# A joined softmax minimum, a third engine for the softmax scale, uneven last pieces and a different warm-up in a two-layer streaming encoder

## The chip, the cores and the metric

The kernel runs on one core of a Trainium2 chip. The core has TensorE (PE in the profile, with its weight loads listed apart as PEld), VectorE (DVE), ScalarE (ACT), GpSimd (POOL), SyncE (SP), whose queue issues all DMAs here, and 16 DMA engines between HBM and the on-chip memory SBUF. TensorE writes its results to the accumulator memory PSUM, which DVE and ACT read. The metric is device time in microseconds, the median of several runs; a profiled execution has its own time and, inside it, the span from the first to the last instruction.

## The reference

One step of a two-layer encoder for 2048 prompt frames and 32 sample frames, all in float32 with 1024 channels. Layer 0 projects the normalised input to queries, keys, values and gates of two attention branches. Branch A has 8 query heads on 2 key heads, sees its own chunk of 64 frames and the two before, and has a learned sink per head; branch B has 8 heads, sees its own chunk and the eight before, and adds a learned bias:

```python
    s = jnp.einsum('bqhgd,bshd->bhgqs', q, k).astype(jnp.float32) * (dh ** -0.5)
    if bias_table is not None:
        s = s + bias.reshape(kvh, g, tq, tk)
    if sinks is not None:
        m = jnp.maximum(jnp.max(s, axis=-1, keepdims=True), sink)
        p = jnp.exp(s - m)
        p = p / (jnp.sum(p, axis=-1, keepdims=True) + jnp.exp(sink - m))
    else:
        p = jax.nn.softmax(s, axis=-1)
    return jnp.einsum('bhgqs,bshd->bqhgd', p.astype(v.dtype), v)
...
    y = jnp.concatenate([oa.reshape(b, t, -1) * jax.nn.silu(ga),
                         ob.reshape(b, t, -1) * jax.nn.silu(gb)], axis=-1)
    return y @ w_out
```

Layer 1 projects to a recurrent branch and a gate, applies a short convolution, a gated linear recurrence along time and an output projection. After each layer comes `x + rms_norm(y) * g`. The outputs are both streams and the new caches and states.

## The kernel before

Data is kept channel-major: channels on the 128 partitions in eight groups, time along the columns. The 2084 columns are cut into six column tiles (five of 352, one of 324), which are handled in three pairs. A dense product multiplies a weight tile of 1024 by 128 with a column tile. For accuracy every operand is split into a high and a low part of reduced precision, and three products (high-high, high-low, low-high) are summed, 24 matmuls for one output tile. Weights come in by DMA (`wst`) and are split on chip: `w_split` (line 485) copies the high part on ACT or DVE and subtracts to get the low part on DVE or POOL (lines 491 to 499). The weights of layer 0's output projection are named wo0.

Attention works in units of 128 queries (32 for the sample). `soft` (line 1231) makes one unit: score products into one of the two PSUM buffers `S`; `reduce` (line 1242), one fused DVE operation a piece, which subtracts the scores from the bias or mask, writes the negated scores to `pt` and keeps their minimum in `nm` (the largest score, negated); the exponent with its sum on ACT (line 1279); a reciprocal on DVE; and the scale of `pt` by the reciprocal and by 0.5 on DVE or POOL (lines 1290 to 1293). The 0.5 belongs to the gate: SiLU is computed as half of `(tanh(z/2) + 1) * z`, and the kernel leaves the half out of the gate and puts it here. In branch B a unit has up to 640 key columns; with five key tiles the scores are two pieces of 320 columns in two buffers, each with its own minimum, and a DVE operation on one column (line 1257) takes the smaller. The sample's units of branch B are two pieces of 272. In branch A a unit has four heads of up to 256 columns, each with its own minimum, which starts from the sink; its scale is four operations. After the scale, TensorE transposes `pt` into the PSUM buffers `T`, ACT copies the high part to `pp`, DVE subtracts for the low part, TensorE multiplies with the values into `O`, and ACT and DVE empty it.

The order of all instructions on all engines is written out by a planner inside the kernel (class `Sched`, lines 166 to 395). Every piece of work is a generator that yields requests: the engine, or a choice of engines with costs in microseconds, and the data and buffers that it needs. The planner keeps a modelled clock for each engine, takes requests by priority, places one on an engine when that engine is modelled to be free within 0.6 us (`LOOK`) and the data is there, and among several engines takes the earliest modelled finish (`pick`, line 323). The dense products have the lowest priority on TensorE and fill what attention leaves. On the chip each engine then runs its list in that order. From the end of attention on, `sch.alone` keeps POOL out of every choice for long stretches.

Layer 1's output projection, `out_part` (line 1730), ends in `fin_out` (line 1629): ACT scales a finished output tile into `m` and squares it, the squares are summed, TensorE sums them over the partitions, ACT takes the root, DVE the reciprocal, and then `m` is multiplied by it and the residual `xt` is added, in channel groups of five and three, on DVE or POOL; SP stores. In the very last column tile the last output tile is computed in two pieces of 162 columns (line 1761), each with its own norm, so that the first piece's norm runs while the second is multiplied.

At the start TensorE multiplies ones by ones eight times (lines 1584 to 1585) before the first data arrives.

Of the kernel before, what the change touches and what calls it, by code (L numbers as in the profile page):

```python
# [12 lines left out]
OP = mybir.AluOpType  # L13
# [38 lines left out]
NQT = 3  # L52
WIN = 3.4133


# [343 lines left out]
def hybrid_kernel(ctx, tc, I, O):  # L399
# [85 lines left out]
    def w_split():  # L485
        for i in range(1, len(WSEQ)):
            if not fresh[i]:
                continue
            wcur[1] = i
            w_use()  # L490
            e, (h, l) = yield R(("A", "V"), [("wst", i), lambda: sch.w.get(wst[i].tensor.name)], [whr, wlr], cost=(0.95, 0.6))
            sch.set(("wt", i))
            s = wst.pop(i)
            if e == "A":
                A.copy(h, s)
            else:
                V.tensor_copy(h, s)
            e, _ = yield R(("V", "G"), [h], cost=(1.14, 2.3))
            ENG[e].tensor_tensor(l, s, f32(h), OP.subtract)
            wstr.release(s)  # L500
            wt[i] = (h, l)
            wleft[i] = 1 if WSEQ[i][0] in ("w0", "wo0") else 2
            if wleft[i] == 2:
                spawn(w_keep(i), PWK)
            sch.set(("W", i), sch.w[l.tensor.name])
# [725 lines left out]
    def soft(run, np_, groups, out, sink=None):  # L1231
# [9 lines left out]

        def reduce(ps, pieces, o0):
            yield R("V", [ps] + ex)
            o = 0
            for i, (_, ks, bv, j) in enumerate(pieces):
                n = ks.stop - ks.start
                V.tensor_tensor_reduce(out=pt[:np_, o0 + o:o0 + o + n], in0=ps[:np_, o:o + n], in1=bv, scale=-1.0,
                                       scalar=BIG if sink is None else nsk[:np_, sink + j:sink + j + 1],
                                       op0=OP.add, op1=OP.min, accum_out=nm[:np_, j:j + 1])
                o += n  # L1250
            Sr.release(ps)
            left[0] -= 1
            if not left[0]:
                if run.bias is not None:
                    run.b_done()
                if sink is None and len(groups) == 2:
                    V.tensor_tensor(nm[:np_, 0:1], nm[:np_, 0:1], nm[:np_, 1:2], OP.min)
                if sink is not None:
                    V.tensor_tensor(r[:np_], sk[:np_, sink:sink + 4], nm[:np_], OP.add)
                sch.set(uid, sch.t["V"] + 0.13)  # L1260

        for gi, pieces in enumerate(groups):
# [5 lines left out]
            for qs, ks, _, _ in pieces:  # L1268
# [3 lines left out]
                o += n  # L1272
            spawn(reduce(ps, pieces, o0), PT)
            o0 += o
# [14 lines left out]
        n = sum(x[1] for x in out)  # L1289
        e, _ = yield R(("V", "G"), [r], cost=(0.06 + n * 0.00053, 0.1 + n * 0.00106))  # L1290
        for j, (o, w) in enumerate(out):
            x = pt[:np_, o:o + w]
            ENG[e].tensor_scalar(x, x, r[:np_, j:j + 1], 0.5, OP.mult, OP.mult)
        for g, t in ((nmr, nm), (smr, ss), (rr4, r)):
# [288 lines left out]
    sch.set(("wst", 1))  # L1583
    for _ in range(NWARM):
        PE.matmul(warmp[:, 0:128], ones, ones, start=True, stop=True)
    psr_.release(warmp)
    spawn(w_first(), -3)
# [33 lines left out]
    class Out:  # L1621


        def __init__(self, b, bi, residual, gi, dst, final):
            self.b, self.bi, self.residual, self.gi, self.dst, self.final = b, bi, residual, gi, dst, final
            self.m = self.sa = None
            self.n, self.left = 0, 2

    def fin_out(S, c, acc, rel, cs):
# [23 lines left out]
        m, half = S.m, S.final and S.bi == 1  # L1653
        pieces = [(o, sw) for o, sw in subs(blk) if cs.start <= o < cs.stop]
        xg = xtr if S.final else xrr
# [16 lines left out]

        def add(o, sw, tm):

            cc = slice(o, o + sw)
            for ks in parts:
                nk = ks.stop - ks.start
                e, _ = yield R(("V", "G"), [lambda: tm[ks.start], lambda: S.xk.get(o)], cost=(0.2 * nk, (FG if S.final else 0.42) * nk))
                xt = S.xt[o]
                ENG[e].tensor_tensor(m[:, ks, cc], m[:, ks, cc], xt[:, ks, :sw], OP.add)  # L1680
                tm[ks.start] = sch.t[e] + 0.13
                if half or ks.stop == KT:
# [4 lines left out]
                                 in_=m[:, sk_, cc])  # L1687
            S.xg.release(xt)
            x2n[S.dst is x2T, S.b] = x2n.get((S.dst is x2T, S.b), 0) + 1
# [6 lines left out]

        for o, sw in pieces:
            cc, tm = slice(o, o + sw), {}
            yield R("V", [r])
            V.reciprocal(r[:, cc], r[:, cc])  # L1700
            for ks in parts:
                nk = ks.stop - ks.start
                e, _ = yield R(("V", "G"), [r], cost=(0.2 * nk, 0.42 * nk))
                ENG[e].tensor_tensor(m[:, ks, cc], m[:, ks, cc], r[:, None, cc].to_broadcast([128, nk, sw]), OP.mult)
                tm[ks.start] = sch.t[e] + 0.13
            spawn(add(o, sw, tm), 0)
        rg.release(r)

    def res_load(S):

        S.xg = xtr if S.final else xrr
        S.xt, S.xk = {}, {}
        for o, sw in subs(2 * S.b + S.bi):
            xt, = yield R("SP", rings=[S.xg])
# [15 lines left out]
    def out_part(b, base, ri, residual, gi, dst, ykey, late=False, late_m=False, final=False):  # L1730
# [7 lines left out]
        for n, (c, bi, wi) in enumerate(order):  # L1738
# [20 lines left out]
            if final and n == 15:  # L1759

                for o, sw in subs(2 * b + bi):
                    if o:
# [359 lines left out]
```

## Time and profile before

| | |
|---|---|
| runs | 1827.22, 1828.31, 1827.37 us; median 1827.37 |
| the profiled execution's own time | 1823.5 us |
| its span | 1821.7 us |
| busy: PE, DVE, ACT, POOL | 1731.5, 1555.3, 996.5, 326.5 us |
| mean granted TensorE clock | 0.988 of full speed |

All lines of a profile carry the line number of one helper (L101), so work is told apart by the names of its tiles: `acc` is a dense product's accumulator; `r0h`, `r0l`, `r1h`, `r1l` are the high and low parts of the activations, `wh` and `wl` of the weights; `S`, `T`, `O`, `pt`, `nm`, `pp` are as above; `rr` holds the reciprocals, `ssm` the sums, `sacc` and `tz` or `tzb` the sums of squares and squares of the norm, `misc` its product over the partitions. The fused reduce is listed as CUSTOM_DVE_ANT_0, followed by a read of its accumulator. Shapes are partitions x elements. In a group's line the first number after the bar is the busy time in us, the second the mean ns of one instruction, and after the second bar stands the engine's idle time before it with what ended it.

### The profile page before, as it was taken

To read this page: it belongs to the slowest core of one execution; us is meant where nothing else is said; L and a number is where in the kernel's file an instruction comes from. 1 tells how busy PE (TensorE), PEld (TensorE's weight loads), DVE (VectorE), ACT (ScalarE), POOL (GpSimd) and SP (SyncE) were. 2 spreads that over 40 slices of the span, in tenths; PEclk is the share of its full clock that TensorE was granted. 3 is DMA by queue.
4 is the path that set the end of the run, shared out by engine and by line. 5 is a ranking of instruction groups with operands and counts; after the bars stand their busy time and mean duration, and the time that the engine had idled before them with its cause. 6 is when DMAs were issued, how large, how long until landed. Compare 5 with 4: busy or idle time off the path is not lost.

```text
span 1821.7 us, 31694 instructions
## 1 busy us (share of the span) xinstructions
PE 1731.5 (95%) x11078; PEld 1671.8 (92%) x11078; DVE 1555.3 (85%) x3330; ACT 996.5 (55%) x2037; POOL 326.5 (18%) x284
## 2 busy tenths in 40 slices
PE   8999999999999999999998999998999999999995
PEld 7999999998999999899997999998999899999995
DVE  9899967899998779998988789899999988798843
ACT  4275543476666416665565344457753675447831
POOL 4332204323322233311222000000011000100002
PEclk8999999999999999999998999999999999999998
DMA  5788766888654368877764985684566735575376
GB/s 179 203 245 265 228 190 196 226 232 237 192 149 141 97 186 248 210 217 195 216 194 122 278 248 168 210 267 147 217 213 217 204 124 174 165 208 171 128 268 193
DMA packets 293576, 362.80 MB, mean 199 GB/s; under 512 B 36308, under 2 KB 244616, under 8 KB 293400
## 3 DMA queue, kind: packets, MB, share of 16 engines
q1 hardware_dynamic: 293416, 360.78, 66.5%
q8 instruction: 87, 1.43, 0.3%
q14 instruction: 73, 0.60, 0.1%
HBM read 255.77 MB, written 107.00 MB: 199 GB/s over the span
## 4 chain that ended last, share of the span: by engine, by line
PE 49%; DVE 29%; DMA 9%; ACT 6%; issue 4%; SPq 1%; POOL 1%; DVEq 0%; ACTq 0%; POOLq 0%
PE acc L101 35%; PE T L101 4%; PE O L101 4%; PE S L101 4%; DVE pt L101 3%; DVE ex L101 3%; DVE m L101 3%; DMA xr<-x2T 3%; DVE ss L101 2%; DVE ti L101 2%; DVE xs L101 2%; DVE s L101 2%; DVE pp L101 2%; DVE eti L101 1%; DVE wl L101 1%
## 5 line engine op out<-in xcount | busy, mean ns | idle before, releaser
L101 PE MATMUL acc<-r0h,wh 128*128 128x352 f32 (+2 forms) x1832 | 592.1, 323 | 6.7 <-ACT tzb L101 2.9
L101 PE MATMUL acc<-r0h,wl 128*128 128x352 f32 (+2 forms) x1832 | 592.2, 323 | 2.9 <-DMA wl<-wo1s 2.9
L101 PE MATMUL acc<-r0l,wh 128*128 128x352 f32 (+2 forms) x1832 | 592.5, 323 | 0.6 <-DVE r0l L101 0.5
L101 PEld LDWEIGHTS acc<-r0h,wh 128*128 128x128 f32 x1832 | 346.2, 189 | 9.3 <-ACT tzb L101 3.1
L101 PEld LDWEIGHTS acc<-r0h,wl 128*128 128x128 f32 x1832 | 346.3, 189 | 4.8 <-DMA wl<-wo1s 4.0
L101 PEld LDWEIGHTS acc<-r0l,wh 128*128 128x128 f32 x1832 | 346.4, 189 | 2.2 <-DVE r0l L101 1.2
L101 PE MATMUL acc<-r1h,wh 128*128 128x352 f32 (+1 forms) x864 | 277.5, 321 | 5.2 <-ACT tz L101 3.6
L101 PE MATMUL acc<-r1h,wl 128*128 128x352 f32 (+1 forms) x864 | 277.0, 321 | 1.6 <-DVE wl L101 1.6
L101 PE MATMUL acc<-r1l,wh 128*128 128x352 f32 (+1 forms) x864 | 276.9, 321 | 0.0
L101 ACT ACTIVATE pt<-pt,nm 128x256 f32<-128x256 f32 (+6 forms) x272 | 169.8, 627 | 61.2 <-DVE nm L101 59.3
L101 ACT CAST pp<-T 128x256 fp32r<-128x256 f32 (+4 forms) x314 | 134.0, 438 | 84.3 <-PE T L101 65.8
L101 PEld LDWEIGHTS acc<-r1h,wh 128*128 128x128 f32 x864 | 162.3, 188 | 6.4 <-ACT tz L101 4.5
L101 POOL TENSOR_SCALAR pt<-pt,rr 128x256 f32<-128x256 f32 (+4 forms) x142 | 100.2, 716 | 366.4 <-DVE rr L101 217.0
L101 PEld LDWEIGHTS acc<-r1h,wl 128*128 128x128 f32 x864 | 162.3, 188 | 1.9 <-DVE wl L101 1.9
L101 PEld LDWEIGHTS acc<-r1l,wh 128*128 128x128 f32 x864 | 162.3, 188 | 0.0
L101 PE MATMUL T<-ident,pt 128*128 128x128 f32 (+2 forms) x864 | 143.3, 274 | 18.0 <-DVE pp L101 10.2
L101 DVE TENSOR_TENSOR pp<-T,pp 128x256 fp32r<-128x256 f32 (+4 forms) x314 | 150.4, 496 | 7.9 <-ACT pp L101 6.0
L101 PE MATMUL O<-pp,vt 128*128 128x256 f32 (+3 forms) x728 | 135.9, 310 | 9.8 <-DVE pp L101 4.7
L101 PEld LDWEIGHTS T<-ident,pt 128*128 128x128 f32 (+2 forms) x864 | 101.7, 140 | 42.4 <-DVE pp L101 19.9
L101 DVE CUSTOM_DVE_ANT_0 pt<-S,bias 128x320 f32<-128x320 f32 (+2 forms) x240 | 108.8, 478 | 17.4 <-PE S L101 14.6
L101 PE MATMUL S<-kk,qa 128*128 128x320 f32 (+5 forms) x376 | 119.7, 333 | 3.8 <-DVE nm L101 3.3
L101 PEld LDWEIGHTS O<-pp,vt 128*128 128x128 f32 (+1 forms) x728 | 107.1, 193 | 16.0 <-DVE pp L101 6.1
(241 smaller groups left out, 3010.1 us busy)
## 6 DMA issues: line engine op xcount, KB each, us to landing
wst<-w_in SPq DMA_DIRECT2D x93, 512.0 KB, 4.4
wst<-wo_in SPq DMA_DIRECT2D x32, 512.0 KB, 5.6
wh<-w1s SPq DMA_DIRECT2D x32, 512.0 KB, 3.8
wl<-w1s SPq DMA_DIRECT2D x32, 512.0 KB, 4.6
wh<-wo1s SPq DMA_DIRECT2D x24, 512.0 KB, 3.9
wl<-wo1s SPq DMA_DIRECT2D x24, 512.0 KB, 4.7
kk<-kB SPq DMA_DIRECT2D x32, 320.0 KB, 4.8
vt<-vB SPq DMA_DIRECT2D x16, 640.0 KB, 4.8
```

Of the source, the lines that this page charges most:

```text
L101: r = fn(*a, **k)
```

## The change

The change has five parts.

1. In a unit without sinks the pieces' minima are joined: the first piece writes its minimum to one column of `nm`, and the second piece's reduce takes that column as its start value, so the operation that took the smaller one is gone. The planner books the second piece's reduce only after the first one's.
2. The 0.5 is taken out of the scale and put into the weights wo0 when they are split. For wo0 the high part is a copy with a factor 0.5, and the low part is one scalar-tensor-tensor operation, on DVE only.
3. The scale of a unit with one output (all of branch B) may also go to ACT, with a modelled cost of 0.197 us and 1 us for 1200 columns.
4. In the last column tile the last output tile is computed in pieces of 240 and 84 columns. Residual tiles are loaded as 176 and 148 columns, so the norm works on pieces of 176, 64 and 84 columns; its multiplications and additions are on DVE only, and it stores six times where it stored four times.
5. The warm-up is four of the old products and sixteen products of 256 columns in the reduced-precision format, some of them on partitions 0 to 63 or 64 to 127 only.

```diff
+LAST, CUT = [(0, 176), (176, 148)], 240
...
+            half = WSEQ[i][0] == "wo0"
+            if half:
+                if e == "A":
+                    A.activation(h, s, AF.Copy, scale=0.5)
+                else:
+                    V.tensor_scalar(h, s, 0.5, None, OP.mult)
+                yield R("V", [h])
+                V.scalar_tensor_tensor(l, s, 0.5, f32(h), OP.mult, OP.subtract)
             else:
-                V.tensor_copy(h, s)
-            e, _ = yield R(("V", "G"), [h], cost=(1.14, 2.3))
-            ENG[e].tensor_tensor(l, s, f32(h), OP.subtract)
...
-        def reduce(ps, pieces, o0):
-            yield R("V", [ps] + ex)
+        def reduce(ps, pieces, o0, gi):
+            on = gi > 0 and sink is None
+            yield R("V", [ps] + ex + ([(uid, 0)] if on else []))
...
+                if sink is None:
+                    j = len(groups) - 1 - gi
                 V.tensor_tensor_reduce(out=pt[:np_, o0 + o:o0 + o + n], in0=ps[:np_, o:o + n], in1=bv, scale=-1.0,
-                                       scalar=BIG if sink is None else nsk[:np_, sink + j:sink + j + 1],
+                                       scalar=nsk[:np_, sink + j:sink + j + 1] if sink is not None else nm[:np_, 1:2] if on else BIG,
                                        op0=OP.add, op1=OP.min, accum_out=nm[:np_, j:j + 1])
...
+            sch.set((uid, gi), sch.t["V"])
...
-                if sink is None and len(groups) == 2:
-                    V.tensor_tensor(nm[:np_, 0:1], nm[:np_, 0:1], nm[:np_, 1:2], OP.min)
...
-        e, _ = yield R(("V", "G"), [r], cost=(0.06 + n * 0.00053, 0.1 + n * 0.00106))
+        e, _ = yield R(("V", "G", "A")[:3 if len(out) == 1 else 2], [r], cost=(0.06 + n * 0.00053, 0.1 + n * 0.00106, 0.197 + n / 1200.0))
...
-            ENG[e].tensor_scalar(x, x, r[:np_, j:j + 1], 0.5, OP.mult, OP.mult)
+            if e == "A":
+                A.activation(x, x, AF.Copy, scale=r[:np_, j:j + 1])
+            else:
+                ENG[e].tensor_scalar(x, x, r[:np_, j:j + 1], None, OP.mult)
...
-    for _ in range(NWARM):
+    for _ in range(NWARM // 2):
         PE.matmul(warmp[:, 0:128], ones, ones, start=True, stop=True)
+    warm2 = Sr.get()
+    full, low, upp = slice(0, 128), slice(0, 64), slice(64, 128)
+    for rows in (full, full) * 2, (low, upp) * 3, (full, low, upp) * 2:
+        for i, x in enumerate(rows):
+            PE.matmul((warm2 if x is upp or x is full and i % 2 else warmp)[:, 0:256], onesr[x], onesr[x, None, :].to_broadcast([x.stop - x.start, 2, 128]), start=True, stop=True)
...
+            self.cells = LAST if final and bi else subs(2 * b + bi)
+            self.n, self.left = 0, 3 if final and bi else 2
...
-        pieces = [(o, sw) for o, sw in subs(blk) if cs.start <= o < cs.stop]
+        pieces = [(max(o, cs.start), min(o + sw, cs.stop) - max(o, cs.start), o) for o, sw in S.cells if o < cs.stop and o + sw > cs.start]
...
-                e, _ = yield R(("V", "G"), [r], cost=(0.2 * nk, 0.42 * nk))
+                e, _ = yield R(("V", "G") if not half else ("V", "V"), [r], cost=(0.2 * nk, 0.42 * nk))
...
-                for o, sw in subs(2 * b + bi):
+                for o, sw in ((0, CUT), (CUT, w - CUT)):
```

More of the change, by code (lines that the diff above doesn't have):

```diff
@@ L493, in w_split @@
             s = wst.pop(i)
-            if e == "A":
-                A.copy(h, s)
-            else:
-                V.tensor_copy(h, s)
-            e, _ = yield R(("V", "G"), [h], cost=(1.14, 2.3))
-            ENG[e].tensor_tensor(l, s, f32(h), OP.subtract)
+            half = WSEQ[i][0] == "wo0"
[6 more added lines that the diff above has]
+                V.scalar_tensor_tensor(l, s, 0.5, f32(h), OP.mult, OP.subtract)
+            else:
+                if e == "A":
+                    A.copy(h, s)
+                else:
+                    V.tensor_copy(h, s)
+                e, _ = yield R(("V", "G"), [h], cost=(1.14, 2.3))
+                ENG[e].tensor_tensor(l, s, f32(h), OP.subtract)
             wstr.release(s)
@@ L1272, in soft @@
                 o += n
-            spawn(reduce(ps, pieces, o0), PT)
+            spawn(reduce(ps, pieces, o0, gi), PT)
             o0 += o
@@ L1289, in soft @@
         n = sum(x[1] for x in out)
-        e, _ = yield R(("V", "G"), [r], cost=(0.06 + n * 0.00053, 0.1 + n * 0.00106))
+        e, _ = yield R(("V", "G", "A")[:3 if len(out) == 1 else 2], [r], cost=(0.06 + n * 0.00053, 0.1 + n * 0.00106, 0.197 + n / 1200.0))
         for j, (o, w) in enumerate(out):
             x = pt[:np_, o:o + w]
-            ENG[e].tensor_scalar(x, x, r[:np_, j:j + 1], 0.5, OP.mult, OP.mult)
+            if e == "A":
+                A.activation(x, x, AF.Copy, scale=r[:np_, j:j + 1])
+            else:
+                ENG[e].tensor_scalar(x, x, r[:np_, j:j + 1], None, OP.mult)
         for g, t in ((nmr, nm), (smr, ss), (rr4, r)):
@@ L1583, in hybrid_kernel @@
     sch.set(("wst", 1))
-    for _ in range(NWARM):
+    for _ in range(NWARM // 2):
         PE.matmul(warmp[:, 0:128], ones, ones, start=True, stop=True)
+    warm2 = Sr.get()
[3 more added lines that the diff above has]
+            PE.matmul((warm2 if x is upp or x is full and i % 2 else warmp)[:, 0:256], onesr[x], onesr[x, None, :].to_broadcast([x.stop - x.start, 2, 128]), start=True, stop=True)
+    Sr.release(warm2)
     psr_.release(warmp)
@@ L1626, in __init__ @@
             self.m = self.sa = None
-            self.n, self.left = 0, 2
+            self.cells = LAST if final and bi else subs(2 * b + bi)
+            self.n, self.left = 0, 3 if final and bi else 2
     def fin_out(S, c, acc, rel, cs):
@@ L1671, in fin_out, with add @@
         parts = (slice(0, 5), slice(5, 8))
-        def add(o, sw, tm):
+        def add(o, sw, at, tm):
             cc = slice(o, o + sw)
@@ L1677, in add @@
                 nk = ks.stop - ks.start
-                e, _ = yield R(("V", "G"), [lambda: tm[ks.start], lambda: S.xk.get(o)], cost=(0.2 * nk, (FG if S.final else 0.42) * nk))
-                xt = S.xt[o]
-                ENG[e].tensor_tensor(m[:, ks, cc], m[:, ks, cc], xt[:, ks, :sw], OP.add)
+                e, _ = yield R(("V", "G") if not half else ("V", "V"), [lambda: tm[ks.start], lambda: S.xk.get(at)],
+                               cost=(0.2 * nk, (FG if S.final else 0.42) * nk))
+                xt = S.xt[at]
+                ENG[e].tensor_tensor(m[:, ks, cc], m[:, ks, cc], xt[:, ks, o - at:o - at + sw], OP.add)
                 tm[ks.start] = sch.t[e] + 0.13
@@ L1687, in add @@
                                  in_=m[:, sk_, cc])
-            S.xg.release(xt)
+            if o + sw == at + dict(S.cells)[at]:
+                S.xg.release(xt)
             x2n[S.dst is x2T, S.b] = x2n.get((S.dst is x2T, S.b), 0) + 1
@@ L1695, in add @@
                 sar.release(S.sa)
-        for o, sw in pieces:
+        for o, sw, at in pieces:
             cc, tm = slice(o, o + sw), {}
@@ L1702, in fin_out @@
                 nk = ks.stop - ks.start
-                e, _ = yield R(("V", "G"), [r], cost=(0.2 * nk, 0.42 * nk))
+                e, _ = yield R(("V", "G") if not half else ("V", "V"), [r], cost=(0.2 * nk, 0.42 * nk))
                 ENG[e].tensor_tensor(m[:, ks, cc], m[:, ks, cc], r[:, None, cc].to_broadcast([128, nk, sw]), OP.mult)
                 tm[ks.start] = sch.t[e] + 0.13
-            spawn(add(o, sw, tm), 0)
+            spawn(add(o, sw, at, tm), 0)
         rg.release(r)
@@ L1712, in res_load @@
         S.xt, S.xk = {}, {}
-        for o, sw in subs(2 * S.b + S.bi):
+        for o, sw in S.cells:
             xt, = yield R("SP", rings=[S.xg])
```

## The prediction

> **What bounds the kernel now.** I read the page first, then the windows of the attention stage, its PE groups, its waits, and last the tail.
>
> ```profile
> span 1821.7 us, 31694 instructions
> PE 1731.5 (95%) x11078; PEld 1671.8 (92%) x11078; DVE 1555.3 (85%) x3330; ACT 996.5 (55%) x2037; POOL 326.5 (18%) x284
> PE 49%; DVE 29%; DMA 9%; ACT 6%; issue 4%; SPq 1%; POOL 1%; DVEq 0%; ACTq 0%; POOLq 0%
> ```
>
> TensorE paces the whole, but 29% of the chain that ended last runs over DVE. The windows split off the attention stage and its end:
>
> ```profile
> 42.00:1002.00 960.00, 925.81 (x6149) 886.00 (x6148) 839.95 (x2292) 533.00 (x1328) 267.65 (x244) 0.99 0.71 200
> 960.00:1002.00 42.00, 36.66 (x226) 33.90 (x227) 33.14 (x90) 23.32 (x53) 10.04 (x6) 0.88 0.38 117
> ```
>
> The columns are window, length, then busy time of PE, PEld, DVE, ACT and POOL, and the granted clock. In the 960 us that the change reshuffles, PE is idle 34 us and DVE busy 87%; the last 42 us have 5.3 us of that idleness and a throttled clock (0.88). PE's groups in 42 to 1012 us (last column: idle before them) say where:
>
> ```profile
> L101 PE MATMUL T<-ident,pt 128*128 128x128 f32 (+2 forms) x864 | 143.3, 274 | 18.0 <-DVE pp L101 10.2 <-DVE rr L101 2.6 <-DVE pt L101 2.0
> L101 PE MATMUL O<-pp,vt 128*128 128x256 f32 (+3 forms) x728 | 135.9, 310 | 9.8 <-DVE pp L101 4.7 <-DVE ot L101 2.7 <-DMA vt<-vBs 1.3
> L101 PE MATMUL S<-kk,qa 128*128 128x320 f32 (+5 forms) x376 | 119.7, 333 | 3.8 <-DVE nm L101 3.3
> ```
>
> These three hold 31.6 us of idle, 25.5 us of it ended by DVE. So the attention edits can gain some 32 us at the very most, and they do it by making DVE earlier.
>
> **1. Joined minimum.** Removed: 104 DVE additions of nothing but the minimum (the 96 of one form, 8 for the sample). The rows and one tile in order of time:
>
> ```profile
> L101 DVE TENSOR_TENSOR nm<-nm 128x1 f32<-128x1 f32 x96 | 30.8, 321 | 3.3
> L101 DVE CUSTOM_DVE_ANT_0 pt<-S,bias 128x320 f32<-128x320 f32 x192 | 87.3, 482 | 14.2 <-PE S L101 12.0 <-POOL pt L101 0.9
> L101 DVE CUSTOM_DVE_ANT_0 pt<-S,amask,nsk 128x256 f32<-128x256 f32 x120 | 51.6, 477 | 2.9 <-PE S L101 2.5
> L101 DVE CUSTOM_DVE_ANT_0 pt<-S,bias 128x256 f32<-128x256 f32 x8 | 3.3, 414 | 0.0
> ```
>
> ```profile
> 792.26 0.49 DVE L101 CUSTOM_DVE_ANT_0 pt<-S,bias 128x320 f32<-128x320 f32 x1
> 792.68 0.08 DVE L101 DVE_READ_ACCUMULATOR2_ANT nm<- 128x1 f32 x1
> 792.68 0.49 DVE L101 CUSTOM_DVE_ANT_0 pt<-S,bias 128x320 f32<-128x320 f32 x1
> 793.09 0.08 DVE L101 DVE_READ_ACCUMULATOR2_ANT nm<- 128x1 f32 x1
> 793.21 0.20 DVE L101 TENSOR_TENSOR nm<-nm 128x1 f32<-128x1 f32 x1
> 793.34 0.41 DVE L101 TENSOR_TENSOR pp<-T,pp 128x256 fp32r<-128x256 f32 x1
> ```
>
> The 321 ns mean is not the price. Two independent reduces start 0.42 us apart; the minimum, which reads the accumulator, starts 0.53 after its reduce (793.21 - 792.68), and the next work 0.13 later. Without it the next work could start 0.42 after the second reduce: 0.66 - 0.42 = 0.24 us saved. What comes instead: the second reduce now reads the first one's accumulator, so it starts 0.53 instead of 0.42 after it (+0.11), and it reads its start value through a pointer, which costs 477 - 414 = 63 ns at 256 columns. Net 0.24 - 0.11 - 0.06 = 0.07 us where the reduces stand side by side, 0.18 where other work fills the gap; 104 tiles give 7 to 19 us of DVE time. No bound goes below zero: the removed operation has more dependent latency than the new wait. In the tiles I looked at they mostly stand side by side, so I take 8 us. Queued behind a second reduce that waits are the pp subtractions that free T, the buffer most waited for; they come 0.11 later inside a tile, 0.07 earlier after it.
>
> **2. The 0.5 leaves the scale, and the scale may go to ACT.** One operation instead of two inside one instruction changes no instruction count; I cost it at nothing, and no work has to hide it. The choice of engine costs more:
>
> ```profile
> L101 DVE TENSOR_SCALAR pt<-pt,rr 128x640 f32<-128x640 f32 x39 | 24.5, 633 | 0.7
> L101 POOL TENSOR_SCALAR pt<-pt,rr 128x640 f32<-128x640 f32 x57 | 55.2, 970 | 237.1 <-DVE rr L101 146.1 <-ACT pp L101 39.0 <-PE O L101 13.3
> L101 ACT ACTIVATE pt<-pt,nm 128x640 f32<-128x640 f32 x96 | 79.9, 832 | 37.4 <-DVE nm L101 35.8 <-DVE pp L101 1.2
> ```
>
> The planner takes the earliest modelled finish: 0.40 us on DVE, 0.78 on POOL, 0.73 on ACT for 640 columns. ACT beats POOL only if it is free within 0.05 us, and it is 56% busy here (533 of 960), so I let it take 25 of POOL's 57 and 10 of DVE's 39. An ACT scale is bounded by the exponent's 832 ns above and by nothing below (it might fall in an ACT pause); 0.83 is nearest, the form being the same. DVE is relieved of 10 x 0.63 = 6 us, and of the stalls behind POOL's 25 scales, which the trace bounds at 0 and 25 x 0.97 = 24 us; I take 4. ACT gains 35 x 0.83 = 29 us. The Trainium skill, page "ScalarE: Activation LUTs", section "Rules for kernel authors", says that a plain multiply belongs on VectorE. The rows agree that an instruction is longer on ACT; by the rule the 10 scales taken from DVE would each lose 0.2 us, the relief below would be 10 us instead of 16 and the attention term about -1, which is rival (a).
>
> **3. wo0 halved at the split.** The high part has a factor instead of a copy; the low part becomes a scalar-tensor-tensor on DVE alone. Of the 24 wo0 splits only those near the end of attention had POOL, since later the planner shuts POOL out:
>
> ```profile
> L101 DVE TENSOR_TENSOR wl<-wst,wh 128x1024 fp32r<-128x1024 f32 x86 | 110.8, 1288 | 2.8 <-ACT wh L101 0.8
> 951.49 2.76 POOL L101 TENSOR_TENSOR wl<-wst,wh 128x1024 fp32r<-128x1024 f32 x1 [3.23 <-ACT wh L101]
> 957.56 2.36 POOL L101 TENSOR_TENSOR wl<-wst,wh 128x1024 fp32r<-128x1024 f32 x1
> 969.98 2.38 POOL L101 TENSOR_TENSOR wl<-wst,wh 128x1024 fp32r<-128x1024 f32 x1 [3.20 <-ACT wh L101]
> ```
>
> Three move: DVE +3 x 1.29 = 3.9 us, less the stalls that these three caused on DVE (0 to 7.5 us, their length). I take +2 us of DVE. The low part's wait for the high part now stands in DVE's queue, ahead of pp subtractions and reduces; the planner books it only once the high part is nearly there.
>
> **Attention at the end.** DVE is relieved of 8 + 6 + 4 - 2 = 16 us. What of it shortens the span? By the chain's shares 29% of DVE's change and 6% of ACT's: -16 x 0.29 + 29 x 0.06 = -2.9 us. Bounds: nothing, or all 16. I take -3.5, a little more than the share, because the waits named above are mostly DVE's.
>
> **4. Tail.** The last column tile now, DVE, POOL, the chain's ACT and the output DMAs:
>
> ```profile
> 1804.24 0.40 ACT L101 ACTIVATE r<-misc,epsT 128x162 f32<-128x162 f32 x1 [1.84 <-PE misc L101]
> 1804.67 1.17 DVE L101 RECIPROCAL r<-r 128x162 f32<-128x162 f32 x1 [4.12 <-ACT r L101]
> 1805.88 1.00 DVE L101 TENSOR_TENSOR m<-m,r 128x810 f32<-128x810 f32 x1
> 1805.92 2.03 POOL L101 TENSOR_TENSOR m<-m,r 128x486 f32<-128x486 f32 x1 [24.10 <-DVE r L101]
> 1807.99 2.67 DVE L101 TENSOR_TENSOR m<-m,r 128x810 f32<-128x810 f32 x1
> 1810.58 3.66 DVE L101 TENSOR_TENSOR m<-m,xt 128x486 f32<-128x486 f32 x2
> 1809.83 4.87 SPq L101 DMA_DIRECT2D yT_out<-m  x4
> yT_out<-m SPq DMA_DIRECT2D x2, 405.0 KB, 6.2
> yT_out<-m SPq DMA_DIRECT2D x2, 243.0 KB, 4.9
> ```
>
> DVE multiplies 810 columns in 1.00 us when it starts beside POOL and in 2.67 when POOL is in the middle: sharing buys nothing here. On DVE alone: reciprocals of 324 columns at 1.17/162 = 7.2 ns are 2.3 us; twice 8 x 324 = 2592 columns at 1.00/810 = 1.23 ns are 6.4 us; with the first reciprocal starting 0.3 us later (240 columns to square and sum) DVE ends at 1804.67 + 0.3 + 8.7 = 1813.7, against 1810.58 + 3.66 = 1814.24. The last DMA goes 0.5 us earlier and carries 3 x 84 columns (126 KB) instead of 243 KB; the two rows give (6.2 - 4.9)/162 = 8 ns a KB, so 0.9 us less to land. That is -1.4 us. PE is out of it: its last products are bound by their weight loads whether 162 or 84 columns wide, and six DMAs instead of four issue in SP's idle time (four took 4.87 us, mostly waiting). Bounds: -2.5 (all of it at the best rates) and +1 (short rows cost what the smaller DMAs save). The Trainium skill, "DMA: Bandwidth & Descriptors", section "Specifications", wants 512 B or more per transfer; pieces of 64 and 84 columns are 256 and 336 B. No row here shows such a store; by the rule the 0.9 us would be lost, and the tail would be -0.5.
>
> **5. Warm-up.** Eight products become four plus sixteen short ones.
>
> ```profile
> 16.00:27.00 11.00, 9.50 (x30) 7.47 (x29) 11.00 (x10) 7.50 (x12) 5.31 (x5) 0.53 0.25 97
> 1.05 3.78 PE L101 MATMUL misc<-onesr 128*128 128x128 f32 x16 [1.05 <-DVE epsT L101]
> 6.49 0.66 PE L101 MATMUL S<-r0h,wh 128*128 128x352 f32 x1 [1.66 <-ACT r0h L101]
> 8.29 7.73 DVE L101 SCALAR_TENSOR_TENSOR r0l<-xt,vec,r0h 128x352 fp32r<-128x352 f32 x7
> 15.58 0.43 PE L101 MATMUL S<-r0l,wh 128*128 128x352 f32 x1 [1.85 <-DVE r0l L101]
> ```
>
> The first row is a window, the rest the timeline. Half of 3.78 us is 1.9; sixteen at the same 0.24 us an instruction (3.78/16) are 3.8: the end is at 6.7, 0.2 after the first product could start at 6.49. That product is covered: its column waits for r0l, which DVE ends at 16.02 either way. What a warmer start could win is the half clock of 16 to 27 us (0.53), 11 x 0.47 = 5 us of TensorE time; but it follows the pause before 15.58 (1.85 us, waiting for r0l), which the warm-up does not touch. Zero; bounds -5 and +0.3.
>
> **Sum.** -3.5 - 1.4 + 0 = -4.9 us on the profiled execution's 1823.5 (span 1821.7 and 1.8 around it): 1818.6. The median of the runs is 1827.37, 3.9 above it, so the median comes to 1822.5.
>
> **Rivals.** (a) *No change that can be told.* 0.2% is 3.7 us, about what a measurement of this kernel separates from no change. PE's order of work is fixed by the planner; if dense products already cover DVE's lag, or if the planner hardly picks ACT, only the tail is left: -1.4, 1826.0. For: PE is idle only 34 us of 960. Against: 25.5 us of that is DVE's. (b) *The bubble at the attention's end closes.* Its 5.3 us of idle and the half clock (0.12 of 42 us, 5 us) go if the last tiles end earlier: -4.9 - 5 = 1817.5. For: the three POOL splits with 2.4 to 2.8 us each stand there. Against: some of its waits are DMA's. (c) *Slower: ACT's queue blocks.* A scale on ACT waits for the reciprocal on DVE; behind it stand the pp casts and exponents, and T is freed late. It decides once DVE runs later than the planner thinks by more than ACT's pause. Held each by half a DVE scale (0.3 us), 35 scales block ACT for 10 us; if half of that reaches PE (+5), the relief is used up (0 instead of -3.5) and the reordering of the planner adds one throttled stretch like the 5 us of (b) in half the cases (+2.5), with the tail's -1.4 it is +6: 1833.5. For: POOL sat 146 us waiting for rr. Against: ACT has 44% free.
>
> **How the numbers follow.** Forecast 0.36, (a) 0.33, (b) 0.15, (c) 0.16. The forecast's own spread (1819 to 1825) loses a few points to "same", (a) and (c) give some back: faster 0.49, same 0.35, slower 0.16. The range leaves out the ends of (b) and (c): 1815.5 to 1831.
>
> **What would show it.** The nm minimum gone, the second reduce 0.53 us after the first and near 0.54 long; 20 to 45 scales on ACT; idle before T and O products under 24 us; no POOL in the last 20 us, and DVE's last addition ending about 8.7 us after the first reciprocal starts (now 1814.24 - 1804.67 = 9.6). Wrong if PE's idle in the stage rises, if ACT waits for rr by tens of us, or if the tail takes longer from its first square root.

## The result and the profile after

| | before | after |
|---|---|---|
| median of six runs each | 1828.32 us | 1842.67 us (1836.11 to 1843.07) |
| ratio | 1 | 1.0073, 95% interval 1.0055 to 1.0090 |
| profiled execution, span | 1823.5, 1821.7 us | 1836.1, 1834.0 us |

The changed kernel is slower by 0.73%, some 13 us by this ratio (the medians themselves differ by 14.4), where 4.9 us less were forecast; the time is above the range too. The profiled execution is the fastest of the six after, 6.6 us under their median, so its profile shows somewhat less than the whole loss. Of the page after, the span and the busy times:

```profile
span 1834.0 us, 31607 instructions
PE 1741.4 (95%) x11086; PEld 1675.3 (91%) x11086; DVE 1536.8 (84%) x3240; ACT 1016.9 (55%) x2071; POOL 343.1 (19%) x241
```

DVE has less to do (1536.8 us against 1555.3), as meant. POOL has 43 instructions fewer than before and 17 us more of busy time (343.1 against 326.5). The two windows of after that answer to those of before, the start and the attention stage:

```profile
16.00:27.00 11.00, 7.99 (x35) 6.64 (x35) 11.00 (x9) 7.36 (x12) 5.51 (x5) 0.84 0.23 89
42.00:1002.00 960.00, 919.26 (x6082) 872.21 (x6081) 819.99 (x2186) 553.85 (x1361) 292.67 (x206) 1.00 0.71 200
```

In the stage DVE is busy 20.0 us less (819.99 against 839.95), and TensorE is idle 40.7 us instead of 34.2: it got through 67 products fewer in the same 960 us. The order of work is new, and attention's last product ends at 985 us instead of 1002, so the two windows do not hold quite the same work. The groups of after in 42 to 1012 us, shapes kept apart, show who became slow:

```profile
L103 POOL TENSOR_SCALAR pt<-pt,rr 128x256 f32<-128x256 f32 x75 | 72.8, 986 | 77.0 <-DVE rr L103 31.1 <-ACT sr L103 9.6 <-PE S L103 7.5
L103 POOL TENSOR_SCALAR pt<-pt,rr 128x640 f32<-128x640 f32 x28 | 56.9, 2031 | 223.3 <-DVE rr L103 115.9 <-PE S L103 65.1 <-PE O L103 18.9
L103 DVE CUSTOM_DVE_ANT_0 pt<-S,bias,nm 128x320 f32<-128x320 f32 x96 | 52.7, 549 | 12.0 <-PE S L103 1.8 <-DVE nm L103 1.0 <-PE acc L103 0.2
...
L103 DVE TENSOR_SCALAR pt<-pt,rr 128x640 f32<-128x640 f32 x43 | 23.6, 552 | 1.1
...
L103 ACT ACTIVATE pt<-pt,rr 128x640 f32<-128x640 f32 x25 | 20.8, 830 | 3.7 <-DVE rr L103 3.5
```

The 256-column row of before:

```profile
L101 POOL TENSOR_SCALAR pt<-pt,rr 128x256 f32<-128x256 f32 x74 | 38.7, 542 | 66.6 <-DVE rr L101 21.6 <-ACT sr L101 13.0 <-PE O L101 8.4
```

POOL's scale of 640 columns takes 2031 ns where it took 970, and of 256 columns 986 where it took 542. DVE's did not slow down: a mean of 552 ns against 633 before, and a median of 553 in both. TensorE's groups in the same window, shapes joined, show where that lands:

```profile
L103 PE MATMUL acc<-r0h,wh 128*128 128x352 f32 (+1 forms) x1234 | 399.8, 324 | 6.2 <-ACT r0h L103 5.7 <-DVE s L103 0.3 <-DVE sr L103 0.2
...
L103 PE MATMUL T<-ident,pt 128*128 128x128 f32 (+1 forms) x864 | 145.9, 276 | 23.6 <-POOL pt L103 12.5 <-DVE pp L103 9.6 <-DVE rr L103 0.4
L103 PE MATMUL O<-pp,vt 128*128 128x256 f32 (+2 forms) x728 | 133.6, 307 | 4.7 <-DVE ot L103 3.3 <-DVE pp L103 1.0
L103 PE MATMUL S<-kk,qa 128*128 128x320 f32 (+5 forms) x376 | 121.1, 336 | 3.2 <-DVE nm L103 2.5
```

The transposes `T` read the scaled `pt`. Before, POOL was not among the three largest releasers of their idle; now it ends 12.5 us of it. The dense products have one wait of 5.7 us for ACT's `r0h` that was not there. The joined minimum on DVE in order of time:

```profile
786.45 0.49 DVE L103 CUSTOM_DVE_ANT_0 pt<-S,bias 128x320 f32<-128x320 f32 x1
786.87 0.08 DVE L103 DVE_READ_ACCUMULATOR2_ANT nm<- 128x1 f32 x1
787.12 0.55 DVE L103 CUSTOM_DVE_ANT_0 pt<-S,bias,nm 128x320 f32<-128x320 f32 x1 [0.17 <-PE acc L103]
787.60 0.08 DVE L103 DVE_READ_ACCUMULATOR2_ANT nm<- 128x1 f32 x1
```

The minimum is gone. The second reduce starts 0.67 us after the first, and what follows it starts at 787.60, 1.15 us after the first reduce; before it was 1.08 (792.26 to 793.34). Over all tiles in which the two reduces stand side by side, the second starts 0.64 us after the first in the median of 65 (0.41 in 75 before), and the next work 1.11 us after it (1.02 before). In 54 of the 65 the profile says that the second reduce waited for DVE's own `nm`; in the tile shown it names a product. The tail of after, ACT's square root, DVE and the stores:

```profile
1815.60 0.46 ACT L103 ACTIVATE r<-misc,epsT 128x240 f32<-128x240 f32 x1 [1.94 <-PE misc L103]
1816.10 1.25 DVE L103 RECIPROCAL r<-r 128x176 f32<-128x176 f32 x1 [4.45 <-ACT r L103]
...
1821.44 3.20 DVE L103 TENSOR_TENSOR m<-m,xt 128x880 f32<-128x880 f32 x6
1822.57 4.42 SPq L103 DMA_DIRECT2D yT_out<-m  x6
```

Counted from the first square root, three steps of before and after: DVE's last addition ends after 10.0 and 9.0 us; the last store has been issued 0.46 us after that (1814.70) and now 2.35 us after that (1826.99); from there to the end of the span it is 7.0 us in both. Together 17.5 and 18.4 us. The profile before is an outlier in the last step, as the other profiles below show.

### The profile page after: what moved, and what is told of

Same layout as the page of the kernel before. It is cut to its first block, busy times and chain, and to the rows that moved or that the text cites. A ratio compares the mean times of both kernels' runs of the same rounds, so it can differ in the third digit from the quotient of the medians.

```text
span 1834.0 us, 31607 instructions
## 1 busy us (share of the span) xinstructions
PE 1741.4 (95%) x11086; PEld 1675.3 (91%) x11086; DVE 1536.8 (84%) x3240; ACT 1016.9 (55%) x2071; POOL 343.1 (19%) x241
## 5 line engine op out<-in xcount | busy, mean ns | idle before, releaser
L103 POOL TENSOR_SCALAR pt<-pt,rr 128x256 f32<-128x256 f32 (+4 forms) x111 | 137.6, 1250 | 316.2 <-DVE rr L103 153.3
L103 PE MATMUL T<-ident,pt 128*128 128x128 f32 (+1 forms) x864 | 145.9, 276 | 23.6 <-POOL pt L103 12.5
L103 PEld LDWEIGHTS T<-ident,pt 128*128 128x128 f32 (+1 forms) x864 | 99.4, 139 | 55.2 <-DVE pp L103 20.8
L103 PE MATMUL O<-pp,vt 128*128 128x256 f32 (+2 forms) x728 | 133.6, 307 | 4.7 <-DVE ot L103 3.3
L103 ACT ACTIVATE m<-acc,vec 128x352 f32<-128x352 f32 (+2 forms) x89 | 48.8, 548 | 142.0 <-PE acc L103 136.9
```

The costliest lines, as they stand in the source:

```text
L103: r = fn(*a, **k)
```

## The experiments

Each ratio is to the kernel before, with its 95% interval. Kernels of one group ran on one chip and share the runs of the kernel before, whose median was 1824.27 us for the first four, 1822.34 for the next four, 1825.01 for the next four and 1823.13 for the last three. "Two operations" is the scale with a second factor, "one operation" without. In the traces every engine runs the same list of work in x1 as in after, and in x2 to x6, x9, x13 and x14 the list of before except where the edit itself adds, drops or moves an operation; x7, x8 and x10 to x12 have orders of their own, and x15 has that of x11.

**1. The scale's form, in the changed kernel and in the old one.** x1 is the changed kernel with a second factor of 1, in the same order of work:

```diff
-                ENG[e].tensor_scalar(x, x, r[:np_, j:j + 1], None, OP.mult)
+                ENG[e].tensor_scalar(x, x, r[:np_, j:j + 1], 1.0, OP.mult, OP.mult)
```

> The changed kernel, with one edit: the softmax scale on DVE and POOL is again a two-operation instruction (times the reciprocal, then times 1.0); the order on every engine stays the changed kernel's. Theory F (the one-operation form is slow on POOL): the 128x640 scale on POOL falls from 1886 ns (median) to about 810, PE's wait for POOL's pt falls from 12.5 us to under 3, and the time falls by 8 to 12 us. Rival O (the planner's new order with ACT's scales costs it): POOL's scale may get shorter, but the time stays within 4 us of the changed kernel's.

x2 is the kernel before with the opposite edit; it leaves out the gate's factor 0.5:

```diff
-            ENG[e].tensor_scalar(x, x, r[:np_, j:j + 1], 0.5, OP.mult, OP.mult)
+            ENG[e].tensor_scalar(x, x, r[:np_, j:j + 1], None, OP.mult)
```

> The kernel before, with its scale as a one-operation instruction on DVE and POOL, nothing else; it leaves out the factor 0.5 of the gate in layer 0. The order on every engine is that of before. Theory F: POOL's 57 scales of 128x640 go from 809 to about 1886 ns and its 74 of 128x256 from 484 to 923, PE waits 10 us or more for POOL's pt, and the kernel is slower by 6 to 14 us. Rival O: within 3 us of before.

x1 took 1829.82 us, 1.0033 (1.0021 to 1.0045); x2 1833.47 us, 1.0050 (1.0028 to 1.0072). POOL's groups of x1:

```profile
L103 POOL TENSOR_SCALAR pt<-pt,rr 128x256 f32<-128x256 f32 x75 | 39.8, 547 | 90.9 <-DVE rr L103 38.5 <-ACT sr L103 13.1 <-PE O L103 8.4
L103 POOL TENSOR_SCALAR pt<-pt,rr 128x640 f32<-128x640 f32 x28 | 26.1, 932 | 245.3 <-DVE rr L103 114.4 <-PE S L103 73.0 <-PE O L103 36.4
```

and its transposes:

```profile
L103 PE MATMUL T<-ident,pt 128*128 128x128 f32 (+1 forms) x864 | 143.3, 275 | 16.0 <-DVE pp L103 13.2 <-POOL pt L103 1.0 <-DVE rr L103 0.4
```

The same of x2, first POOL's groups, then the transposes:

```profile
L101 POOL TENSOR_SCALAR pt<-pt,rr 128x640 f32<-128x640 f32 x57 | 114.6, 2013 | 195.5 <-DVE rr L101 116.4 <-ACT pp L101 32.4 <-PE T L101 18.6
...
L101 POOL TENSOR_SCALAR pt<-pt,rr 128x256 f32<-128x256 f32 x74 | 70.8, 972 | 52.2 <-DVE rr L101 13.9 <-ACT sr L101 9.5 <-PE O L101 8.7
```

```profile
L101 PE MATMUL T<-ident,pt 128*128 128x128 f32 (+2 forms) x864 | 147.0, 277 | 31.2 <-POOL pt L101 16.7 <-DVE pp L101 8.2 <-DVE pt L101 3.0
```

The form alone turns 932 ns into 2031 in one kernel and 970 into 2013 in the other. With it the idle before `T` goes from 16.0 to 23.6 us (7.6 more) and from 18.0 to 31.2 (13.2 more); the time by 1.0073/1.0033, 0.40% or 7.3 us, and by 0.50% or 9.2 us. The form's cost is shown from both sides, in a fixed order. By these middle values it is the larger part of the 13 us; the two intervals together leave the 0.40% anywhere from 0.2 to 0.6%. The Trainium skill, "GPSIMD Engine Reference", section "4.1 Engine selection", sets GpSimd against VectorE for elementwise work and calls an operation with one input roughly line-rate there. Here the two-operation form is 1.5 times DVE's mean and the one-operation form 3.7 times (2031 to 552), so for this operation the measurement decides.

**2. The tail, and the warm-up, each alone in the old kernel.** x3 has part 4 of the change (the lines of the diff from `LAST, CUT` and from `self.cells` on):

```diff
+LAST, CUT = [(0, 176), (176, 148)], 240
...
-                for o, sw in subs(2 * b + bi):
+                for o, sw in ((0, CUT), (CUT, w - CUT)):
```

> The kernel before with the last column tile's new pieces (240 and 84 columns, norm on DVE alone, six stores) and nothing else. My prediction for this part was -1.4 us from the first square root to the end of the span (17.5 us before). Rival S (the stores set the end: six issues in a row on SP, most rows under 512 B): DVE ends about 1 us earlier but the span ends 0.5 to 1.5 us later.

x4 has part 5:

```diff
-    for _ in range(NWARM):
+    for _ in range(NWARM // 2):
...
+    for rows in (full, full) * 2, (low, upp) * 3, (full, low, upp) * 2:
```

> The kernel before with the new warm-up and nothing else. My prediction was 0 (-5 to +0.3 us). In the changed kernel the half clock at the start is one window of 3.4 us instead of 10.2, and its dense work is 0.8 us ahead at 54 us; if that is the warm-up's doing and nothing takes it back, -0.8 us; if later work is paced by something else, 0.

x6 keeps the old pieces of 162 columns and puts their multiplications and additions on DVE alone:

```diff
...
-                e, _ = yield R(("V", "G"), [r], cost=(0.2 * nk, 0.42 * nk))
+                e, _ = yield R(("V", "V") if half else ("V", "G"), [r], cost=(0.2 * nk, 0.42 * nk))
```

> The kernel before with the last column tile's norm on DVE alone but its old pieces of 162 columns and its old four stores. If DVE alone was the gain and the pieces with their six stores the loss: DVE's last addition ends about 1 us earlier after the first square root (before 10.0 us, changed kernel 9.0), and the span ends 0.5 to 1.5 us earlier after it (before 17.5, changed kernel 18.4). If DVE alone is no help, both stay within 0.3 us of before.

x3 took 1827.11 us, 1.0013 (1.0001 to 1.0026); x4 1820.80 us, 0.9993 (0.9976 to 1.0009); x6 1820.94 us, 0.9998 (0.9984 to 1.0012). The tail of x6:

```profile
1803.61 0.40 ACT L101 ACTIVATE r<-misc,epsT 128x162 f32<-128x162 f32 x1 [1.84 <-PE misc L101]
...
1808.81 3.94 SPq L101 DMA_DIRECT2D yT_out<-m  x4
1810.14 2.15 DVE L101 TENSOR_TENSOR m<-m,xt 128x486 f32<-128x486 f32 x3
```

From the first square root to the end of the span the seven profiles with the old tail took 15.7 to 17.5 us (mean 16.1), the seven with the new one 17.2 to 18.4 (mean 17.8), and the three with the old pieces on DVE alone 15.3 to 15.8 (mean 15.5). So the new tail costs 1.7 us and DVE alone is worth 0.6. The first square root itself comes 0.25 us later with 240 columns than with 162, counted from the first product of the last output tile; from there to the end of the span the new tail costs 2.0 us (means 23.4 and 21.4). In x6 DVE ends 8.7 us after the square root and the last store's issue 0.46 us later: with four stores SP is done with DVE, with six it is 2.35 us behind. From the last issue to the end of the span the means are 5.7 us in the old tail, 6.4 in the new one and 6.4 in the three with the old pieces on DVE alone.

**3. The joined minimum in a fixed order.** The planner can reorder everything behind a request that changes. x5 therefore issues the joined form but books the old operations with the planner, so that every engine keeps the order of before:

```diff
+                if two:
+                    to = dict(k, accum_out=nm[:np_, 1 - gi:2 - gi], scalar=nm[:np_, 1:2] if gi else BIG)
+                    nc.vector.tensor_tensor_reduce(**to)
+                    sch.book("V", "tensor_tensor_reduce", [k["out"], k["accum_out"]], [k["in0"], k["in1"]], (), k)
...
-                    V.tensor_tensor(nm[:np_, 0:1], nm[:np_, 0:1], nm[:np_, 1:2], OP.min)
+                    sch.book("V", "tensor_tensor", [nm[:np_, 0:1]], [nm[:np_, 0:1], nm[:np_, 1:2]], (), {})
```

> The kernel before with the minima joined, and the planner still booking the old operations, so the order on every engine is that of before without the 104 one-column operations. My prediction's step: second reduce 0.53 us after the first, 7 to 19 us of DVE time saved, and so a gain of 0 to 4 us. Rival W (the second reduce waits for two things, and the trace of the changed kernel has it about 0.64 to 0.68 us after the first): first reduce to the work after the second takes 1.11 us instead of 1.01, DVE loses 5 to 10 us, and the kernel is 0 to 4 us slower than before.

x5 took 1821.17 us, 0.9997 (0.9983 to 1.0012). Its attention stage and its transposes:

```profile
42.00:1002.00 960.00, 927.48 (x6134) 887.25 (x6134) 825.83 (x2187) 532.67 (x1328) 267.63 (x244) 0.99 0.70 199
```

```profile
L101 PE MATMUL T<-ident,pt 128*128 128x128 f32 (+2 forms) x864 | 143.8, 275 | 18.7 <-DVE pp L101 11.1 <-DVE pt L101 4.1 <-POOL pt L101 1.6
```

DVE is busy 14.1 us less than before (825.83 against 839.95) with the same work in the same order otherwise, the transposes wait for DVE as long as before, and the time does not move. Less busy is not sooner done here: where the two reduces stand side by side and the next work is ready (71 tiles), the next work starts 0.10 us later after the first reduce than before, in the median; only in 20 tiles with other work between the reduces does it come sooner, 0.13 us counted from the second reduce. Idle time took the place of the minimum, as rival W of the expectation had it.

**4. ACT as a third engine, with the planner free.** x7 is x1 without the choice of ACT:

```diff
-        e, _ = yield R(("V", "G", "A")[:3 if len(out) == 1 else 2], [r], cost=(0.06 + n * 0.00053, 0.1 + n * 0.00106, 0.197 + n / 1200.0))
+        e, _ = yield R(("V", "G"), [r], cost=(0.06 + n * 0.00053, 0.1 + n * 0.00106, 0.197 + n / 1200.0))
```

> The changed kernel with the two-operation scale, and the scale not allowed on ACT. If ACT's scales are what is left of the loss (two-operation scale: 1.0033 of before), this comes to 1.000 to 1.002 of before. If the joined minimum and the tail are, it stays at 1.002 to 1.005.

x8 is x1 with separate minima:

```diff
-            yield R("V", [ps] + ex + ([(uid, 0)] if on else []))
+            yield R("V", [ps] + ex)
...
+                if sink is None and len(groups) == 2:
+                    V.tensor_tensor(nm[:np_, 0:1], nm[:np_, 0:1], nm[:np_, 1:2], OP.min)
```

> The changed kernel with the two-operation scale and the two minima taken separately again, as before; ACT may still take scales. If the joined minimum is what is left of the loss, this comes to 0.999 to 1.002 of before. If ACT's scales are, it stays at 1.002 to 1.005.

x7 took 1825.40 us, 1.0008 (0.9991 to 1.0025); x8 1850.33 us, 1.0139 (1.0118 to 1.0159). The two kernels x8 and x1 differ by 1.06%, some 19 us, far more than the one-column operations; the longest of TensorE's waits in x8 is nearly of that size (us in total, times, longest):

```profile
PE acc L103 <- ACT r1h L103: 16.4, 1, 16.4
```

It is one wait, in layer 1, where no softmax is left: this order brings ACT's split of one activation tile late. x1 has no such wait. So a small edit can cost more through the order than by itself.

**5. How much the order alone moves the time.** The same meaningless nudge in three kernels: the planner's extra price for an operand of one column in an operation on DVE goes from 0.030 to 0.032 us (the expectation of x15 calls it GpSimd's price, but `cost` adds it for DVE alone). The work to be done is unchanged; its order is not, nor which of two allowed engines takes an operation.

```diff
-PEMA, VPTA = 0.0, 0.03
+PEMA, VPTA = 0.0, 0.032
```

x10 is x1 with it, x11 the kernel before with it, x12 x7 with it.

> The changed kernel with the two-operation scale and ACT allowed (1.0033 of before), with one meaningless nudge to the planner: the booked price of a one-column operand on DVE is 0.032 instead of 0.03 us. The work is the same, the order differs. Theory A (ACT's scales themselves cost 4 to 6 us): slower than the run without ACT under the same nudge by 3 to 7 us. Rival L (which order the planner happens to find decides): the difference has either sign, and this kernel moves by 3 us or more against its unnudged form.

> The kernel before with the same nudge and nothing else. Rival L: its time moves by 2 us or more (0.1% or more) although no work changes. If the planner's orders are all alike, within 0.1% of before.

> The changed kernel with the two-operation scale and no scale on ACT (1.0008 of before), with the same nudge. Theory A: it stays below the nudged kernel with ACT by 3 to 7 us. Rival L: either sign.

x10 took 1853.00 us, 1.0150 (1.0126 to 1.0173); x11 1815.20 us, 0.9943 (0.9921 to 0.9965); x12 1832.75 us, 1.0051 (1.0032 to 1.0071). Against their own kernels that is +1.2% (1.0150/1.0033), -0.6% and +0.4% (1.0051/1.0008). x10 again has a single wait of 16.4 us for `r1h`, and one of 9.3 us for the low part of a weight. A difference of 0.25% between x1 and x7 says nothing on ACT against such a spread; it had to be measured in a fixed order.

**6. ACT's scales and wo0 in the fixed order.** x13 has the order of before on every engine but issues on ACT what the planner gave to POOL:

```diff
+            if e == "G" and len(out) == 1:
+                nc.scalar.activation(x, x, AF.Copy, scale=r[:np_, j:j + 1])
+                sch.book("G", "tensor_scalar", [x], [x, r[:np_, j:j + 1]], (x, x, r[:np_, j:j + 1], 0.5, OP.mult, OP.mult), {})
+            else:
+                ENG[e].tensor_scalar(x, x, r[:np_, j:j + 1], 1.0, OP.mult, OP.mult)
```

> Before's order of work, engine by engine, with one difference: the 66 scales of units with one output that stood on GpSimd are issued on ScalarE instead. All scales are the two-operation form with a second factor of 1, so the factor 0.5 of the warm-up rows is left out. Theory A (a scale on ScalarE costs the products beside it, because the activations that TensorE waits for stand behind it): TensorE's waits for ScalarE at its first-layer products grow, and the time is 3 to 7 us over the kernel before. Rival L (the order of the work decides, not the engine of the scale): within 2 us of the kernel before.

(The factor that x13 leaves out is the gate's 0.5 of part 2; the expectation misnames it.) x14 halves wo0 at its split (high part and low part as in the change), with the old operations booked, and has the two-operation scale with a factor of 1, so that, unlike what its expectation says, the 0.5 is there:

```diff
...
+            if half:
+                nc.vector.scalar_tensor_tensor(l, s, 0.5, f32(h), OP.mult, OP.subtract)
+                sch.book(e, "tensor_tensor", [l], [s, f32(h)], (l, s, f32(h), OP.subtract), {})
...
```

> Before's order, with only the halving of wo0 at the split (its low rows on VectorE, 3 of them from GpSimd) and the two-operation scale with a second factor of 1, the factor 0.5 left out. Both theories: within 2 us of the kernel before; were it over 3 us slower, part of what is left of the loss with the two-operation scale would be wo0's.

x13 took 1822.96 us and x14 1823.26 us, both 1.0008 (0.9994 to 1.0022 and 1.0023). What ACT did in x13, its group and its wait for the reciprocal:

```profile
L1294 ACT ACTIVATE pt<-pt,rr 128x640 f32<-128x640 f32 x57 | 47.3, 833 | 12.9 <-DVE rr L101 12.8
```

```profile
ACT pt L1294 <- DVE rr L101: 17.6, 18, 4.9
```

57 scales of 640 columns moved to ACT, more than twice the 25 of the change; ACT stood 17.6 us before such scales, and the time is the same within the interval. Neither ACT's scales nor wo0 show a loss of their own; the intervals leave room for up to 4 us each.

**7. The parts that do not lose, together.** x9 is x5 with the warm-up of x4 and the tail of x6; x15 is x9 with the nudge. Their lines are those shown above.

> The order of the kernel before up to the last column tile, with the parts that did no harm alone: the joined minimum (0.9997 of before), the new warm-up (0.9993), and in the last column tile the norm on DVE alone with the old pieces of 162 columns (0.9998). If their small gains add, 0.998 to 0.9995 of before (1 to 4 us); if each was nothing, 0.999 to 1.001.

> The joined minimum, the new warm-up products and the last tile on VectorE alone in the old pieces, with the scale as before, and the planner's price of one GpSimd operation raised from 0.03 to 0.032 us. If the gain of the nudge and that of the parts add (0.57% and 0.41%), 0.990 of the kernel before; if the order decides anew, anywhere from 0.99 to 1.01.

x9 took 1817.34 us, 0.9959 (0.9944 to 0.9973); x15 1805.58 us, 0.9910 (0.9892 to 0.9927), which beats both kernels. The transposes of x15:

```profile
L101 PE MATMUL T<-ident,pt 128*128 128x128 f32 (+2 forms) x864 | 143.5, 275 | 12.3 <-DVE pp L101 6.4 <-DVE pt L101 5.2 <-POOL pt L101 0.2
```

12.3 us of idle, against 18.0 before; in x11, which has the same order without the three parts, it is 16.3. The parts' own ratios (0.9997, 0.9993, 0.9998) would make 0.9988, and x9's 0.9959 is below that; each part's interval is about 0.15% wide to either side, so either they are worth more than could be told of each alone, or more together; that was not separated. x15 is near the product of 0.9959 and 0.9943, 0.9902: against x11 the three parts are worth 0.33% (0.9910/0.9943), against before 0.41%, so they help together in both orders.

## Why the prediction was wrong

**The step that failed: "One operation instead of two inside one instruction changes no instruction count; I cost it at nothing".** The instruction stayed and its time on POOL doubled. Of the 13 us, 7 to 9 are this by the middle values of x1 and x2; the idle time before `T` grew with it by as much or more (7.6 and 13.2 us). The prediction had quoted the rows of the old form (970 and 633 ns) and priced the new form by them without a row that showed it. It bounded the new scale on ACT and the new minimum from both sides, but not this form. No rival had it.

**The attention sum, -3.5.** Three of its sizes were good: POOL lost 29 scales of 640 columns where 25 were taken, ACT's take 830 ns (0.83 taken), and the second reduce takes 549 ns (540 taken); three low parts of wo0 left POOL in x14, as counted. ACT took 25 of these scales, not 35, and DVE gained 4 (39 to 43) instead of losing 10. What failed is the relief of DVE itself. The 14.1 us of x5 look like the 16 of the prediction, but they are busy time: 71 x 0.10 us later and 20 x 0.13 us sooner make DVE's queue some 4.5 us longer over the tiles counted, an estimate from the medians of x5 and before. The price, "29% of DVE's change" by the chain's shares, is therefore not tested by x5: no run here makes DVE's queue shorter in a fixed order. A chain's share says where the path ran; that it is also what the path loses when DVE does less was assumed, and so was that the subtractions' freeing of `T` waits for the engine's turn. The waits for `pp` stay in x5 (10.2 us before, 11.1).

**The joined minimum, 0.07 us a tile where the reduces are adjacent.** The second reduce was to start 0.53 us after the first and starts 0.64 after it in the median tile, so that the next work comes 0.10 us later instead of 0.07 earlier. The 0.53 was read from another operation behind a reduce, the one-column minimum; no row showed a reduce behind a reduce whose minimum it takes. "No bound goes below zero" is the sentence that failed. Why it is 0.11 us more than for the one-column operation was not tried.

**The tail, -1.4.** The step on DVE is right: 8.7 us from the first reciprocal were forecast and 1824.64 - 1816.10 = 8.5 measured. TensorE is out of it, as said: its last products start 112 to 113 ns apart whether 84, 162 or 240 columns wide (149 ns at 324). Wrong are the two steps behind DVE. "Six DMAs instead of four issue in SP's idle time": they do not, the last issue ends 2.35 us after DVE instead of 0.46 (1.9 us lost). "0.9 us less to land" for 126 KB instead of 243: 7.0 us in these two profiles, and in the means over all profiles 0.8 us more (6.4 against 5.7). Together the tail costs about 2 us, above the bound of +1. The Trainium skill, "DMA: Bandwidth & Descriptors", section "Specifications", wants 512 B or more per transfer; the prediction let that rule take the 0.9 us away and no more. The traces agree in direction: the 126 KB in short rows took as long to land as the 243 KB of x6, x9 and x15 (6.4 us in both means). That row length is the cause was not separated from the number of stores and their spacing.

**Warm-up, zero.** Right in the time (x4, 0.9993). The clock in 16 to 27 us was 0.53 before and is 0.84 in after and in x4; but over all profiles it is 0.53 to 0.85 with the old warm-up and 0.55 to 0.88 with the new one, so that it does not tell the two apart, and x4 shows no gain that can be told.

**The rivals.** (c) named 1833.5 us, the nearest to the time, by ACT's blocked queue; its wait was 5.4 us in after, against the 10 of that rival, and x13 shows 17.6 us of it without a loss that can be told. So (c) was near by luck: the reason that it gives did not make the loss. (a) is what most of the parts did one by one. (b)'s bubble did not close: in 960 to 1002 us TensorE is idle 6.0 us after against 5.3 before, though the clock there is 0.94 instead of 0.88. What all of them priced too low is the planner: (c) alone had a term for its reordering, +2.5 us, while an edit that touches attention's requests or their prices can make the order new, and a nudge alone moved the time by -0.6, +0.4 and +1.2%. A range of 0.85% was too narrow for that, whatever the parts cost.

**The signs.** Of what the prediction named, these came: the minimum gone, the second reduce near 0.54 us long, 20 to 45 scales on ACT, no POOL in the last 20 us. These did not: the second reduce 0.53 us after the first, and under 24 us of idle before `T` and `O` (23.6 + 4.7 = 28.3). Two of its three signs of being wrong came: more idle time of TensorE in the stage (40.7 against 34.2 us) and a longer tail.

**What the 13 us are.** 7.3 us the scale's form (after against x1), 2.4 us the tail (x3, 0.13%; 2.0 by the profiles), and 3 to 4 us left, all by middle values whose intervals are some 2 to 4 us wide to either side. The rest is time which ACT's scales, wo0, the joined minimum and the warm-up do not show in a fixed order, and which lies within the spread of orders. The single wait for `r0h` (5.7 us in after, 6.0 in x1) is of that size, but x7 has one of 7.2 us and a ratio of 1.0008; so which place in the order costs the rest stays open.

## What to carry to other kernels

Price each instruction by the form in which it will run on each engine that may take it: dropping an operand can make it slower, and a row of the old form is no bound for the new one. In a kernel whose order comes from a planner, measure each part in a fixed order (issue the new instruction, book the old one), and measure a meaningless nudge first, to know how far the order alone moves the time. Price a removed operation by the time from start to start on its engine's queue, and not by its busy time: an operation that now waits for the one ahead of it can leave the engine less busy and its queue no shorter.

## What the runs showed of the hardware

- POOL's multiply of `pt` by a value per row takes 932 to 970 ns for 128x640 with a second constant factor and 2013 to 2031 without; for 128x256 542 to 547 and 972 to 986. DVE shows no such step: means of 552 to 633 ns for 128x640 in all four kernels (before, after, x1, x2), and a median of 553 in each.
- A reduce on DVE that takes the minimum of the reduce ahead of it starts 0.64 us after that one (median of after, x1 and x5), an independent one 0.41 (before); the one-column minimum started 0.53 after its reduce in the tile of before.
- One wait of TensorE among some 11,000 products, the 16.4 us for `r1h` in x8 and x10, is 0.9% of the time; two different edits brought it about.
- Six stores from SP took 4.42 us to issue, where the four of before took 4.87 us, mostly waiting for DVE, and 3.94 in x6; SP's last issue ended 2.35 us after DVE's last addition with six, and 0.46 us with four.
- Products of 84, 162 and 240 columns at the end of the kernel started 112 to 113 ns apart, those of 324 columns 149 ns (before and after).
